# Gate steps in sparse attention, and where a chunked scan computes its decays and norm factors

## The chip, the core and the metric

The kernel runs on one core of a Trainium2 chip. A core has five engines that run their own instruction streams side by side: TensorE (PE in the profile; its weight loads are PEld), VectorE (DVE), ScalarE (ACT), GpSimd (POOL) and SyncE (SP), which here issues nearly all DMAs. They meet through semaphores, in SBUF (on-chip memory) and in PSUM (the banks that TensorE accumulates into). The metric is the device time of one execution in microseconds (us).

## What is computed

One layer of a hybrid decoder: three token mixers side by side on the same normalised input (a Mamba-2 scan, stick-breaking attention, sparse attention), merged by sigmoid gates, then a convolved gated MLP. SEQ is 1024, D_MODEL 1024, one batch. What the change touches of the reference:

```python
def ssd_chunked(x, dt, a, bmat, cmat):      # 8 chunks of 128 tokens, 4 groups of 4 heads
    def step(state, inp):
        x_c, dt_c, b_c, c_c = inp
        acum = jnp.cumsum(dt_c * a, axis=1)
        seg = acum[:, :, None] - acum[:, None, :]
        decay = jnp.exp(jnp.where(tri, seg, -jnp.inf))
        cb = jnp.einsum('btgn,bsgn->btsg', c_c, b_c)
        w = cb[..., None] * decay * dt_c[:, None]
        y = jnp.einsum('btsgh,bsghp->btghp', w, x_c)
        y = y + jnp.einsum('btgn,bghpn->btghp', c_c, state) * jnp.exp(acum)[..., None]
        ...
# after it, per group of 256 channels:
    yg = yg * lax.rsqrt(jnp.mean(yg * yg, axis=-1, keepdims=True) + NORM_EPS)

# sparse attention, per query: 64 compressed keys give an importance for 16 blocks of 64 keys
        imp_pad = jnp.pad(p_cmp.sum(axis=2), ((0, 0), (0, 0), (0, 0), (1, 0)))
        imp = (imp_pad.reshape(bsz, g, NSA_QBLK, nb, ratio).sum(axis=-1)
               + jnp.pad(imp_pad[..., ratio::ratio], ((0, 0), (0, 0), (0, 0), (0, 1))))
        imp = jnp.where(valid, jnp.where(forced, BIG, imp), NEG)
        _, idx = lax.top_k(imp, n_sel)

# merge
    gm = jax.nn.sigmoid(merge_gate).reshape(bsz, s, 3, D_MODEL)
    mixed = gm[:, :, 0] * (y_ssm @ w_br_ssm) + gm[:, :, 1] * (y_sb @ w_br_sb) + gm[:, :, 2] * (y_nsa @ w_br_nsa)
```

## The kernel before

Activations are channel-major: a tile is 128 channels by 512 tokens (one half of the sequence). A float32 product is made of three passes on TensorE, with each operand split into a rounded part and a remainder (`hi`, `lo`): hi·hi, hi·lo, lo·hi. A **unit** is 128 output channels of the input projection: two halves, each 8 steps (one per 128 input channels) of three 128x512 matmuls into a PSUM bank named `dense`. `load_w` (L263) fetches a unit's weights by SP, ScalarE makes `whi` (L270), GpSimd `wlo` (L271).

The program runs through stages: the normalised input and the token-major projections; sparse attention (`nsa_stage`); stick-breaking attention (`sb_stage`, four heads); the scan (`ssd_stage`, four groups q of 8 chunks c); the merge, the output projection and the MLP (`tail_stage`). The 24 units of the merge gates depend on nothing but the input and are needed only in the tail, so they serve as **fill**: `Fill.take(n)` puts n of their steps between the matmuls of a stage. `N_GATES`, `SB_GATES` and `SSD_GATES` (L165 to L167) say how many gate units each stage gets. A gate unit ends each half with three ScalarE operations (the sigmoid, L245 to L247) and a store to DRAM.

**Sparse attention.** The outer loop (L944) goes over n. In one turn it interleaves three coroutines: the scores and values of query block n (`attend`), the row maxima of block n+1 (`maxima`) and the compressed branch of block n+2 (`compressed`). Blocks are (g, i): two head groups, eight query blocks i. TensorE's order in this stage is the order of the code; other engines are ordered by the Tile scheduler, as everything is in the later stages. Per inner step, the loop takes two fill steps where no key block is due (`b is None`), else one if the two other coroutines had nothing to do (L976 to L979). Query block i has i+1 key blocks in the selected branch and min(i,4)+1 in the windowed one; the loop has at least `NSA_SLOTS` = 9 inner steps, so from i = 4 on (10 to 13 key blocks) no inner step is without one. `maxima` ends with a transpose of the running maxima through PSUM and a copy into rows 96 to 127 of Q1 (L861 to L863); the next turn's first score needs them. `compressed` exponentiates and normalises scores against 64 compressed keys (`cp`), from i = 4 on reduces them to the importance of 16 blocks and picks eight (L784 to L796), transposes `cp`, copies it out (`pT`, L803), multiplies it with the compressed values into the same PSUM bank (L807) and multiplies the result by its gate into `yacc` (L809). The bank `ps_b` has one buffer.

**The scan.** For group q, `front(c)` makes the decays of a chunk (L1167): DMA brings `cum`, the cumulated log decays of four heads broadcast over partitions; VectorE subtracts the row's own value and clips at 0, one operation of 128x128 per head (L1174); ScalarE exponentiates the four together (L1176); GpSimd multiplies with C·B into `W` (L1198) and makes `Cd` (L1181). Four TensorE operations go into `ps_t` (two buffers), read by `cb`, `xdt`, `Bt` and `xe` (L1194 to L1204). `back(c)` multiplies into `ps_b` and `ps_o`, updates `state` (L1225) and the rows of x (L1228). After each chunk `fill.take` gives two halves of units (one in the last group): the projection of the next group, then gates. Dense halves of the projection rotate over three banks, two of `psd` and one `ps_s` (class `Banks`); gate halves use `psd` alone. At the end of a group `rsqrt_mean` (L235) makes the norm factors: Ln and Exp by ScalarE into SBUF, then one Newton step by VectorE, all tiles but the first source in SBUF, and L1248 multiplies them into the rows.

## Time and profile before

| what | value |
|---|---|
| time, median of 3 runs | 2200.53 us (2199.61 to 2202.32) |
| the profiled execution's own time | 2200.72 us |
| its span, first to last instruction | 2199.0 us |
| mean granted TensorE clock | 0.994 |
| VectorE busy | 1352.9 us (62%) |
| ScalarE busy | 1264.8 us (58%) |
| GpSimd busy | 1094.2 us (50%) |
| sparse attention, about | 195 to 525 us of the span |
| stick-breaking attention, about | 525 to 907 us |
| scan, about | 907 to 1250 us |

The profile lists for each instruction its start and duration, and for an engine that sat idle the instruction that ended the wait ("idle before, releaser"). Durations of neighbouring instructions overlap: a 128x512 matmul shows 0.39 us, but the next one starts 0.23 us later. So start-to-start times are used for what work costs, and the idle column for what a wait costs.

### The profile page before, as it was taken

The numbers are of one execution on the slowest core, as the hardware profiler recorded it, in microseconds if no ns is written. First come the engines' busy times: TensorE is split into PE (matmuls) and PEld (weight loads), VectorE is DVE, ScalarE is ACT, GpSimd is POOL, SyncE is SP. The second block draws the span as 40 slices with busy tenths as digits, with TensorE's granted clock in tenths as the row PEclk, the third lists the DMA queues.
The fourth block names the chain that finished last, engine by engine and source line by source line (L and its number), as shares of the span: only waits on it lengthen the run. The fifth ranks groups of instructions, "written<-read, shape, count | busy, mean of one in ns | idle before, by whom it ended". The sixth has DMA issues, their size and how long they took to land. (4 is left out here: it accounts for less than half of the span.)

```text
span 2199.0 us, 30216 instructions
## 1 busy us (share of the span) xinstructions
PE 2139.4 (97%) x10697; PEld 1739.8 (79%) x10697; DVE 1352.9 (62%) x2538; ACT 1264.8 (58%) x2328; POOL 1094.2 (50%) x797
## 2 busy tenths in 40 slices
PE   7999999999999999999999899999999999999997
PEld 7997666767887878777887688888888888888887
DVE  8433774672277676848486743326876666666677
ACT  7134676666466677655555422135686666676564
POOL 3212576566233333343434427455577777765753
PEclk9999999999999999999999999999999999999999
DMA  5223212200201111222222455244444444486533
GB/s 199 85 84 94 68 37 68 72 13 30 66 34 53 48 41 46 82 82 82 73 81 87 139 208 184 96 141 166 140 139 158 163 144 149 136 275 200 186 114 115
DMA packets 127079, 240.73 MB, mean 109 GB/s; under 512 B 29328, under 2 KB 43472, under 8 KB 126928
## 3 DMA queue, kind: packets, MB, share of 16 engines
q1 hardware_dynamic: 126064, 238.06, 33.2%
q8 instruction: 84, 1.38, 0.3%
q10 hardware_dynamic: 864, 0.75, 0.1%
q14 instruction: 67, 0.55, 0.1%
HBM read 179.45 MB, written 59.31 MB: 109 GB/s over the span
## 5 line engine op out<-in xcount | busy, mean ns | idle before, releaser
L271 POOL TENSOR_TENSOR wlo<-wraw,whi 128x1024 fp32r<-128x1024 f32 (+1 forms) x118 | 273.8, 2322 | 403.8 <-ACT whi L270 379.9
L206 PE MATMUL dense<-h_hi,whi 128*128 128x512 f32 x896 | 361.2, 403 | 2.7 <-ACT sa L1070 2.7
L206 PE MATMUL dense<-h_hi,wlo 128*128 128x512 f32 x896 | 352.2, 393 | 0.0
L206 PE MATMUL dense<-h_lo,whi 128*128 128x512 f32 x896 | 351.7, 393 | 0.0
L270 ACT ACTIVATE whi<-wraw 128x1024 fp32r<-128x1024 f32 (+1 forms) x118 | 117.8, 999 | 186.6 <-PE dense L206 156.3
L887 POOL TENSOR_TENSOR wT_lo<-wT,wT_hi 128x512 fp32r<-128x512 f32 x132 | 168.9, 1290 | 87.2 <-ACT wT_hi L886 77.1
L206 PEld LDWEIGHTS dense<-h_hi,whi 128*128 128x128 f32 x896 | 169.3, 189 | 38.7 <-ACT sa L1070 3.1
L206 PE MATMUL dense<-lo,whi 128*128 128x512 f32 x512 | 199.5, 390 | 0.0
L206 PE MATMUL dense<-hi,whi 128*128 128x512 f32 x512 | 199.4, 392 | 0.0
L206 PE MATMUL dense<-hi,wlo 128*128 128x512 f32 x512 | 197.8, 389 | 0.0
L206 PEld LDWEIGHTS dense<-h_hi,wlo 128*128 128x128 f32 x896 | 168.9, 188 | 36.3 <-issue 0.5
L206 PEld LDWEIGHTS dense<-h_lo,whi 128*128 128x128 f32 x896 | 169.3, 189 | 32.2 <-issue 0.9
L1087 POOL TENSOR_TENSOR s_lo<-sa,s_hi 128x512 fp32r<-128x512 f32 (+2 forms) x48 | 53.8, 1125 | 151.1 <-ACT s_hi L1086 148.1
L206 PE MATMUL dense<-x,uhi 128*128 128x512 f32 x360 | 116.7, 389 | 0.0
L876 ACT ACTIVATE wT<-ps_s 128x512 f32<-128x512 f32 x132 | 78.5, 595 | 63.7 <-PE ps_s L206 58.9
L206 PEld LDWEIGHTS dense<-hi,whi 128*128 128x128 f32 x512 | 96.1, 188 | 20.7 <-issue 0.7
L206 PEld LDWEIGHTS dense<-lo,whi 128*128 128x128 f32 x512 | 96.1, 188 | 20.7 <-issue 0.7
L206 PEld LDWEIGHTS dense<-hi,wlo 128*128 128x128 f32 x512 | 96.1, 188 | 20.5 <-issue 0.5
L316 DVE SCALAR_TENSOR_TENSOR u<-dense,pv,u 128x511 f32<-128x511 f32 (+1 forms) x140 | 102.0, 741 | 5.4 <-ACT u L312 4.2
L886 ACT ACTIVATE wT_hi<-wT 128x512 fp32r<-128x512 f32 x132 | 82.2, 629 | 16.6 <-POOL wT L878 15.1
L206 PE MATMUL ps_s<-Q,K 128*128 128x512 f32 x264 | 83.6, 398 | 4.3 <-DVE Q L863 4.1
L1198 POOL TENSOR_TENSOR W<-dec,cb 128x512 f32<-128x512 f32 x32 | 42.5, 1334 | 81.6 <-DVE cb L1194 49.6
(483 smaller groups left out, 5798.7 us busy)
## 6 DMA issues: line engine op xcount, KB each, us to landing
wraw<-in_wfm SPq DMA_DIRECT2D x62, 512.0 KB, 3.7
wraw<-in_wup SPq DMA_DIRECT2D x52, 512.0 KB, 3.8
g_d<-gate_e SPq DMA_DIRECT2D x48, 256.0 KB, 2.1
ge<-g_d SPq DMA_DIRECT2D x24, 512.0 KB, 3.9
m_d<-u SPq DMA_DIRECT2D x44, 256.0 KB, 2.1
u<-m_d SPq DMA_DIRECT2D x36, 256.0 KB, 3.2
wraw<-in_wdn SPq DMA_DIRECT2D x33, 256.0 KB, 3.1
cum<-acum_d SPq DMA_DIRECT2D x32, 256.0 KB, 3.5
```

What stands on the lines that cost most here:

```text
L206: i = f(*a, **k)
L270: act(hi, raw, AF.Copy)
L271: (eng or (V if tiles else P)).tensor_tensor(lo, raw, fl(hi), op=OP.subtract)
L316: end = V.scalar_tensor_tensor(o[:, d:], ps[:, :512 - d], taps[d], o[:, d:], op0=OP.mult, op1=OP.add)
L876: act(w.rearrange("p h q -> p (h q)"), pz, AF.Exp)
L886: act(hi, wf, AF.Copy)
L887: P.tensor_tensor(lo, wf, fl(hi), op=OP.subtract)
L1087: (P if SB_SLO else V).tensor_tensor(s_lo[:, c0:], a[:, c0:], fl(s_hi[:, c0:]), op=OP.subtract)
L1198: P.tensor_tensor(W, dec, cb[:, None, :].to_broadcast([128, 4, 128]), op=OP.mult)
```

## The change

- `N_GATES` is 13 instead of 12. The cuts of the later stages move by one; stick-breaking attention keeps one gate unit for each of its first three heads, and the scan's group q = 1 has one gate unit instead of two.
- In a turn of the sparse loop with more than nine key blocks, two fill steps are taken ahead of the first score. `compressed` yields True for i < 4 between the copy `pT` and the product that reads it, and the loop then takes one more step there.
- The importance of the 16 blocks is one reduction over overlapping windows of five (stride four) of a buffer with four zero columns behind it, in place of a reduction over four, an addition of the neighbour and a multiplication by a mask; the mask that is added (0, 1e30 or -1e30) stays.
- The decays' difference is made by ScalarE: Relu(acum - cum) for each head, and the exponential takes the opposite sign.
- In groups q < 3 of the scan, the norm factors are made in the PSUM bank that holds the sum of squares, and multiplied into the rows half by half. The last group keeps `rsqrt_mean`.

```diff
-N_GATES = 12
-SB_GATES = (12, 13, 14, 15, 15)
-SSD_GATES = (15, 17, 19, 20, 24)
+N_GATES = 13
+SB_GATES = (13, 14, 15, 16, 16)
+SSD_GATES = (16, 18, 19, 20, 24)
...
+    imps = [wk.tile([128, 68], F32, name=f"imp{n}", bufs=1) for n in range(2)]
+    for t in imps:
+        P.memset(t, 0.0)
...
+    def windows(imp):
+        w = imp[:, 0:64].rearrange("p (b r) -> p b r", r=4)
+        return bass.AP(tensor=w.tensor, offset=w.offset, ap=[list(w.ap[0]), list(w.ap[1]), [1, 5]])
...
-            imp = wk.tile([128, 64], F32, name="imp")
-            V.tensor_reduce(imp, p.rearrange("p h n -> p n h"), axis=AX, op=OP.add)
+            imp = imps[i % 2]
+            V.tensor_reduce(imp[:, 0:64], p.rearrange("p h n -> p n h"), axis=AX, op=OP.add)
             im = wk.tile([128, 16], F32, name="im")
-            iv = imp.rearrange("p (b r) -> p b r", r=4)
-            V.tensor_reduce(im, iv, axis=AX, op=OP.add)
-            V.tensor_tensor(im[:, 0:15], im[:, 0:15], iv[:, 1:16, 0], op=OP.add)
-            V.tensor_tensor(im, im, fa[:, i, 0, :], op=OP.mult)
+            V.tensor_reduce(im, windows(imp), axis=AX, op=OP.add)
             V.tensor_tensor(im, im, fa[:, i, 1, :], op=OP.add)
...
         act(pT.rearrange("p a b -> p (a b)"), pt[:, :256], AF.Copy)
-        yield
+        yield i < 4
...
+        if nb > NSA_SLOTS:
+            fill.take(NSA_FILL[0])
         for m, b in enumerate(blocks):
...
-            idle = next(ga, 0) == 0
+            step = next(ga, 0)
+            idle = step == 0 and step is not False
...
-            fill.take(NSA_FILL[0] if b is None else NSA_FILL[1] + idle)
+            fill.take((NSA_FILL[0] if b is None else NSA_FILL[1] + idle) + (step is True))
...
             for h in range(4):
-                V.tensor_scalar(dec[:, h, :], cum[:, h, :], E.acum[:, c, 4 * q + h:4 * q + h + 1], 0.0,
-                                op0=OP.subtract, op1=OP.min)
-            act(dec, dec, AF.Exp)
+                act(dec[:, h, :], cum[:, h, :], AF.Relu, scale=-1.0, bias=E.acum[:, c, 4 * q + h:4 * q + h + 1])
+            act(dec, dec, AF.Exp, scale=-1.0)
...
-            E.rsqrt_mean(z1[:, s], z0[:, s], ps, 256)
+            if q == 3:
+                E.rsqrt_mean(z1[:, s], z0[:, s], ps, 256)
+                continue
+            v = z1[:, s]
+            V.tensor_scalar(v, ps, 1.0 / 256, EPS, op0=OP.mult, op1=OP.add)
+            act(ps, ps, AF.Ln, scale=1.0 / 256, bias=E.eps)
+            act(ps, ps, AF.Exp, scale=-0.5)
+            V.tensor_tensor(v, v, ps, op=OP.mult)
+            V.scalar_tensor_tensor(v, v, -0.5, ps, op0=OP.mult, op1=OP.mult)
+            V.scalar_tensor_tensor(ps, v, 1.5, ps, op0=OP.add, op1=OP.mult)
+            for n in range(2):
+                V.scalar_tensor_tensor(xs[n][:, s], xs[n][:, s], pvc(PV_SSM, 2 * q + n), ps, op0=OP.mult,
+                                       op1=OP.mult)
         for n in range(2):
-            V.scalar_tensor_tensor(xs[n], xs[n], pvc(PV_SSM, 2 * q + n), z1, op0=OP.mult, op1=OP.mult)
+            if q == 3:
+                V.scalar_tensor_tensor(xs[n], xs[n], pvc(PV_SSM, 2 * q + n), z1, op0=OP.mult, op1=OP.mult)
```

**Where instructions move.** TensorE, sparse attention, the start of the turn for query block 4 of the first head group. Before: the transposes of the maxima (`top`) stand directly ahead of the first score, whose operands are the tiles Q1 and Q2 and the keys K.

```order
L206 MATMUL ps_o<-wT_hi,V_hi 65x512
L206 MATMUL ps_o<-wT_hi,V_lo 65x512
L206 MATMUL ps_o<-wT_lo,V_hi 65x512
L206 MATMUL ps_t<-tab,top_1811 128x128 x4
L206 MATMUL ps_s<-Q_2674,K_0_1078 128x512
L206 MATMUL ps_s<-Q_2675,K_0_1080 128x512
```

The same place with the change:

```order
L206 MATMUL ps_t<-tab,top_1815 128x128 x4
L206 MATMUL dense<-h_hi,whi 128x512
L206 MATMUL dense<-h_lo,whi 128x512
L206 MATMUL dense<-h_hi,wlo 128x512
L206 MATMUL dense<-h_hi,whi 128x512
L206 MATMUL dense<-h_lo,whi 128x512
L206 MATMUL dense<-h_hi,wlo 128x512
L206 MATMUL ps_s<-Q_2687,K_0_1078 128x512
L206 MATMUL ps_s<-Q_2688,K_0_1080 128x512
```

Two steps of a gate unit, six matmuls, stand between the transposes and the score that waits for their copy. This happens in the eight turns of i = 4 to 7 in both head groups; in the eight of i = 0 to 3 one step comes between the transpose of `cp` and its product with VC. Those 24 steps are 8 that stood behind the stage's last attention step before, and the 16 of the thirteenth unit.

VectorE at the start of the scan, group q = 0, chunks 0 to 2, before (`dec` the decays, the `row` lines with `dense` or `ps_s` the convolution of the group's own projection, `xe` the operand that frees a `ps_t` bank):

```order
L1228 SCALAR_TENSOR_TENSOR row_8511<-row_8511,pv,ps_o 128x128
L1228 SCALAR_TENSOR_TENSOR row_8722<-row_8722,pv,ps_o 128x128
L1196 TENSOR_TENSOR xdt<-ps_t,dt_t 128x256
L1174 TENSOR_SCALAR dec<-cum,acum 128x128 x4
L540 SCALAR_TENSOR_TENSOR row_9615<-ps_s,pv,halo 128x3
L542 SCALAR_TENSOR_TENSOR row_9615<-ps_s,pv,row_9615 128x511
L1204 TENSOR_TENSOR xe<-ps_t,dte 128x256
```

and with the change:

```order
L1234 SCALAR_TENSOR_TENSOR row_8557<-row_8557,pv,ps_o 128x128
L1234 SCALAR_TENSOR_TENSOR row_8768<-row_8768,pv,ps_o 128x128
L1202 TENSOR_TENSOR xdt<-ps_t,dt_t 128x256
L528 TENSOR_TENSOR row_9538<-row_9538,half 128x512
L540 SCALAR_TENSOR_TENSOR row_9661<-ps_s,pv,halo 128x3
L1210 TENSOR_TENSOR xe<-ps_t,dte 128x256
```

The four `dec` operations between `xdt` and `xe` are gone from VectorE, as are sixteen ahead of them. On ScalarE they stand here, with the change (`dec` from `cum` is the Relu, `dec` from `dec` the exponential, `half` the sigmoid of the projection's SiLU):

```order
L1208 ACTIVATE Bt<-ps_t 128x128 x2
L1181 ACTIVATE dec<-cum,acum 128x128 x8
L1182 ACTIVATE dec<-dec 128x512
L534 ACTIVATE row_9661<-dense,pv 128x512
L536 ACTIVATE halo<-dense,pv 128x3
L1182 ACTIVATE dec<-dec 128x512
L1185 ACTIVATE cum<-cum 128x512
L245 ACTIVATE half<-row_9538 128x512
L1181 ACTIVATE dec<-cum,acum 128x128 x4
L246 ACTIVATE half<-half 128x512
L1181 ACTIVATE dec<-cum,acum 128x128 x4
L1182 ACTIVATE dec<-dec 128x512
```

The first two chunks' eight Relus stand together ahead of an eviction of the projection (`row` from `dense`); the next eight come between the operations of a sigmoid. No instruction that loads an activation table is added.

## The prediction, made before the changed kernel was run

> **What bounds the kernel now.** First the page and the busy time by stage, to see which engine sets the time and where it is not busy.

> ```profile
> span 2199.0 us, 30216 instructions
> PE 2139.4 (97%) x10697; PEld 1739.8 (79%) x10697; DVE 1352.9 (62%) x2538; ACT 1264.8 (58%) x2328; POOL 1094.2 (50%) x797
> ...
> 195.00:525.00 330.00, 316.21 (x1739) 227.33 (x1738) 211.08 (x538) 215.94 (x409) 199.79 (x192) 1.00 0.17 50
> ...
> 907.00:1250.00 343.00, 332.49 (x1831) 264.90 (x1830) 236.30 (x546) 180.99 (x309) 142.62 (x87) 1.00 0.28 89
> ```

> In the window rows the second number is the stretch, the third TensorE's busy time. TensorE is the bound: it idles 2199.0 - 2139.4 = 59.6 us. The change removes no matmul from it; it moves gate steps and shortens what other engines do. So it can win no more than TensorE waits in the stages it touches: 330 - 316.2 = 13.8 us in sparse attention, 343 - 332.5 = 10.5 us in the scan. Next, who ended those waits (total, times, longest), first sparse attention, then the scan:

> ```profile
> PE ps_s L206 <- DVE Q L863: 4.1, 4, 1.3
> PE ps_b L206 <- ACT pT L803: 3.0, 4, 1.0
> PE ps_b L206 <- DVE yacc L809: 1.9, 2, 1.0
> ...
> PE ps_b L206 <- DVE state L1225: 5.0, 4, 1.7
> PE ps_t L206 <- DVE xe L1204: 4.2, 1, 4.2
> PE ps_o L206 <- DVE row L1228: 1.3, 1, 1.3
> ```

> The first two are the places where the change inserts steps; the third is behind the importance on VectorE; the last three are the scan's whole idle time.

> **Gate steps ahead of scores and behind the copy pT.** One of the four pT waits on TensorE's timeline, with the dense steps behind it:

> ```profile
> 229.28 0.39 PE L206 MATMUL ps_b<-tab,cp 128*128 128x128 f32 x2
> 230.67 0.71 PE L206 MATMUL ps_b<-VC,pT 128*128 128x128 f32 x4 [1.01 <-ACT pT L803]
> 231.14 0.48 PE L206 MATMUL dense<-h_hi,whi 128*128 128x512 f32 x1
> 231.46 0.40 PE L206 MATMUL dense<-h_lo,whi 128*128 128x512 f32 x1
> 231.69 0.39 PE L206 MATMUL dense<-h_hi,wlo 128*128 128x512 f32 x1
> ```

> A step costs 3 x 0.23 = 0.69 us; the first dense matmul behind another kind takes 0.32 instead of 0.23, so a new place for a step costs about 0.09 us more. One step covers 0.69 us of each of four pT waits (3.0 us in all, longest 1.0): about 2.5 us go, 0.5 stay. Two steps, 1.38 us, cover each of four score waits (4.1 us, longest 1.3): 4.1 us go, or 3.9 where a copy comes a little later. Sixteen new places cost 16 x 0.09 = 1.4 us. The steps themselves are no extra work: 8 of the 24 come from the stage's end, 16 from the scan's second group, where they ran without a wait before.

> The 24 steps are three halves of units: nine sigmoid operations, one and a half weight splits by ScalarE and by GpSimd, three stores and one or two weight loads on SP's queue, all earlier than before. ScalarE is busy 215.9 of 330 us here and GpSimd 199.8, so there is room; what queues behind a sigmoid operation is a pT, Q or score copy for up to some 0.6 us. I charge 0.5 us for all of it, with bounds 0 and 4 (eight turns by one such operation less what their own two steps cover).

> **Importance.** VectorE, in the turn that makes one of the two yacc waits:

> ```profile
> 267.64 0.52 DVE L788 TENSOR_TENSOR im<-im,imp 128x15 f32<-128x15 f32 x1
> 268.42 0.99 DVE L789 TENSOR_TENSOR im<-im,fa 128x16 f32<-128x16 f32 x1
> 270.58 0.41 DVE L809 TENSOR_TENSOR yacc<-ps_b,sg 128x256 f32<-128x256 f32 x1
> 271.24 0.16 DVE L792 MAX8 top<-im 128x8 f32<-128x16 f32 x1
> ...
> 271.85 0.15 DVE L794 MATCH_REPLACE8 left<-top,im 128x16 f32<-128x16 f32 x1
> ...
> 271.04 0.66 PE L206 MATMUL ps_b<-tab,qd 128*128 128x128 f32 x4 [0.96 <-DVE yacc L809]
> ```

> L788 and L789 go: 1.5 us ahead of yacc here. In the new order the maximum and the replacement come ahead of it instead, 0.16 + 0.15 and some 0.1 to load the values to match, so yacc comes about 1.1 us earlier and the 0.96 us go; 1.6 of the two waits' 1.9 us is my value, bounds 0 and 1.9. The reduction reads 80 numbers instead of 64, at nothing: VectorE is not waited for there.

> Sparse attention: 2.5 + 3.9 + 1.6 - 1.4 - 0.5 = **6.1 us** gained, bounds 1 and 10.

> **Decays by ScalarE.** The largest single wait, with the engines around it:

> ```profile
> 919.45 2.38 POOL L271 TENSOR_TENSOR wlo<-wraw,whi 128x1024 fp32r<-128x1024 f32 x1 [0.31 <-ACT whi L270]
> 921.79 1.26 POOL L1198 TENSOR_TENSOR W<-dec,cb 128x512 f32<-128x512 f32 x1
> 923.01 1.26 POOL L1181 TENSOR_TENSOR Cd<-cum,row 128x512 f32<-128x512 f32 x1
> ...
> 919.61 4.94 DVE L1174 TENSOR_SCALAR dec<-cum,acum 128x128 f32<-128x128 f32 x4
> ...
> 925.85 0.90 PE L206 MATMUL ps_t<-tab,row 128*128 128x128 f32 x3 [4.18 <-DVE xe L1204]
> ...
> 920.00:930.00 10.00, 5.82 (x34) 4.59 (x33) 9.93 (x20) 5.62 (x13) 4.27 (x3) 0.83 0.28 80
> ...
> L1174 DVE TENSOR_SCALAR dec<-cum,acum x128: 269/276/2393, 907.0 to 1235.1; 128x128 f32<-128x128 f32 x128
> ...
> L1174 DVE TENSOR_SCALAR dec<-cum,acum 128x128 f32<-128x128 f32 x128 | 60.4, 525 | 7.2 <-POOL W L1198 6.5 <-DMA cum<-acum_d 0.7
> ```

> Four decays take 4.94 us where 4 x 0.276 (the median) would be 1.1: they last as long as GpSimd's three operations beside them. xe waits behind them in VectorE's queue, and TensorE's transposes wait for xe's bank: 4.18 us. After the wait TensorE runs slower for a while: its granted clock is 0.83 over these 10 us (the number after the five engines), so another 10 x 0.17 = 1.7 us are lost. Without the decays VectorE has nothing of that kind ahead of xe: 16 more that stood before are gone too, at 0.525 us some 8 us. What is late next is W, by way of ScalarE: its eight first Relus. They have no row; the nearest are these:

> ```profile
> L1202 ACT ACTIVATE Bt<-ps_t 128x128 f32<-128x128 f32 x28 | 7.2, 269 | 7.7 <-PE ps_o L206 4.2 <-DVE xdt L1196 3.5
> L1096 ACT ACTIVATE sz<-sz 128x256 f32<-128x256 f32 x16 | 6.7, 418 | 0.0
> L1096 ACT ACTIVATE sz<-sz 128x512 f32<-128x512 f32 x24 | 15.1, 628 | 1.7 <-DVE sz L1095 0.9
> ```

> A 128x128 copy out of PSUM takes 0.27 us; from SBUF, 0.42 at 256 columns is the upper bound, and less 128 x (628 - 418) / 256 it is 0.31, my value. A chunk's four take 1.2 us (1.1 to 1.7). VectorE took 1.1 at best and 2.1 on average, so W comes no later, and in the new order 20 dense matmuls stand between the first two products with W. I count the 4.2 + 1.7 = **5.9 us** as gained, bounds 2 and 6.

> [...]

> **Norm factors in PSUM.** They count in the last group, where VectorE still makes those of the group before. Its Newton step and the end of the scan on TensorE:

> ```profile
> 1210.09 2.89 DVE L240 TENSOR_TENSOR row<-row,row 128x512 f32<-128x512 f32 x1
> ...
> 805.75 0.68 DVE L1073 TENSOR_TENSOR sa<-ps_s,sa 128x512 f32<-128x512 f32 x1
> ...
> 1213.89 0.67 PE L206 MATMUL ps_b<-xe,Bt 128*128 128x256 f32 x2 [0.80 <-DVE state L1225]
> 1223.65 0.67 PE L206 MATMUL ps_b<-xe,Bt 128*128 128x256 f32 x2 [1.38 <-DVE state L1225]
> ...
> 1236.21 0.70 PE L206 MATMUL ps_b<-xe,Bt 128*128 128x256 f32 x2 [1.12 <-DVE state L1225]
> 1239.65 0.67 PE L206 MATMUL ps_b<-xe,Bt 128*128 128x256 f32 x2 [1.71 <-DVE state L1225]
> 1242.67 0.66 PE L206 MATMUL ps_o<-W,xdt 128*64 128x128 f32 x8 [1.33 <-DVE row L1228]
> ```

> L240 with both sources in SBUF took 2.89 us; the same shape with one source in PSUM takes 0.68 (L1073). With 2.2 us from there, and each chunk's decays, the first two waits (0.80 and 1.38) go. The last three have no gate step left between chunks: PSUM product, state, product again. The fourth and fifth, 3.0 us, stay; of the third, half goes. **2.8 us** gained, bounds 0 and 6.3.

> **What is taken away.** Group q = 1 loses a gate unit, 16 x 0.69 = 11 us of cover for its end and the start of q = 2. Group q = 2 has had one gate unit before, and at its end TensorE's wait column is empty until 1213.89; so I cost it at little. But both ps_s banks are now held until their half is multiplied into the rows: six VectorE operations of L1073's size, 4.1 us a half, 8.2 for both, and states and rows are queued between. The third bank of the next group's projection is one of them, and in the new order 32 dense matmuls (7.4 us) and two chunks' products stand ahead of its first use. I charge **1 us**, bounds 0 and 5 (a 3 us wait with the slower matmuls behind it).

> The stages before and behind keep their order up to noise: the stick-breaking stage's waits and the tail's I take as they are.

> **The sum**: 6.1 + 5.9 + 2.8 - 1.0 = 13.8 us. From the profiled execution's own 2200.72 us (span 2199.0 and 1.7 around it), which is the median of the runs shown plus 0.2: 2186.9, so 2186.7 for a median, say **2187 us**. About 0.2% (4.4 us) is what a measurement can tell from no change.

> **Rivals.**
> - All waits at these places go, those at the scan's end too: 13.8 + 10.5 + 1.7 less the 1.4 of new places: 2176 us. For it: steps give every engine slack. Against: the scan's end has nothing to put between.
> - The waits of sparse attention are moved, not removed: VectorE is so busy from i = 4 on that the next score or transposes wait instead. For: five smaller kinds of wait stand behind the three shown, 13.8 - 9.0 = 4.8 us. Gain 1 there: 2192 us.
> - The ps_s banks hold up the projection at two group ends, 4 us each: 2194 us. For: by the terms above there is hardly a margin. Against: only every third bank is one, and TensorE has other work in its queue ahead of it.
> - Slower: ScalarE becomes the scan's bound. In the last group the decays' 1.2 us a chunk join exponentials, gates and weights:

> ```profile
> 1200.00:1240.00 40.00, 34.99 (x216) 26.61 (x216) 34.26 (x86) 22.64 (x40) 20.73 (x15) 1.00 0.31 106
> ```

> ScalarE (sixth number) is busy 22.6 of 40 us; five chunks add 6, leaving 11 free. It decides if evictions queued behind Relus free banks later by over 1 us in most of 32 chunks: 24 us lost, and the scan's 8.7 not gained, 6.1 kept: some 2218 us; half of that would be 2206. [...]

> **Chances.** Forecast 0.56 (2181 to 2192); all waits go 0.12; moved waits 0.13; banks 0.11; ScalarE 0.08. Faster by over 0.2% (under 2196): all of the first two, most of the next two, 0.87; same 0.07; slower 0.06. The range, 2177 to 2196, reaches from the first rival to just behind the third, and leaves out the slower case and the edges.

> **What the next profile would show.** Right: the waits for Q L863 and yacc gone, hardly a pT wait left; stick-breaking attention starting about 5 us later (11 of the thirteenth unit less 6.1), the scan ending about 14 earlier; no wait over 2 us between 907 and 1200; the fourth and fifth wait at the scan's end still there. Wrong: dense waits ended by ScalarE (half, gate_e) in the scan, a ps_s matmul waiting for VectorE, or the score waits still there with steps ahead of them.

## The result, and the profile after

The changed kernel takes 2177.83 us (median of 4 runs, 2176.78 to 2178.68) against 2200.56 us before on the same chips: ratio 0.9895, 95% interval 0.9882 to 0.9908, so 22.7 us less. A later set of runs of it gave 2177.89 us, 0.9897 (0.9883 to 0.9910). The forecast was 2187 us, 13.8 us less.

The head of the page of the profiled execution (2176.78 us), as it was shown of before:

```profile
span 2174.9 us, 30180 instructions
PE 2133.0 (98%) x10697; PEld 1736.5 (80%) x10697; DVE 1287.2 (59%) x2400; ACT 1301.7 (60%) x2456; POOL 1093.7 (50%) x799
```

TensorE runs the same 10697 matmuls. VectorE has lost 65.7 us of busy time and ScalarE has gained 36.9: 128 decays that cost VectorE 60.4 us have gone to ScalarE.

Next, what TensorE waited for in sparse attention (195 to 523 us; total, times, longest), changed kernel:

```profile
PE ps_o L206 <- ACT oT L904: 1.2, 5, 0.4
PE ps_t L206 <- DVE mx L856: 1.1, 2, 0.6
PE ps_b L206 <- DVE cp L785: 1.0, 1, 1.0
PE ps_t L206 <- DVE top L856: 0.9, 3, 0.4
```

The scores' waits for Q (4.1) and the waits for pT (3.0) and yacc (1.9) are gone, all of them. Only mx has grown by more than 0.1 us (0.3 before). The same view of the scan, with nothing left out:

```profile
PE ps_o L206 <- DVE row L1234: 1.3, 1, 1.3
PE ps_b L206 <- DVE state L1231: 0.9, 1, 0.9
```

10.5 us of waits have become 2.2; both that are left are at the scan's end, at 1215 and 1218 us.

Where the 24.1 us between the two spans lie is read from TensorE's timeline, at the first operation of each stage: the first transposes of `q_in`, the first stick-breaking score, the first product with `W`, the last group of products with `Cd`. Before:

```profile
169.99 0.38 PE L206 MATMUL ps_b<-tab,q_in 128*128 128x128 f32 x2
590.01 0.87 PE L206 MATMUL ps_s<-row,row 128*128 128x256 f32 x6
913.39 0.66 PE L206 MATMUL ps_o<-W,xdt 128*64 128x128 f32 x8
1243.13 0.64 PE L206 MATMUL ps_o<-Cd,state 128*64 128x128 f32 x8
```

After:

```profile
168.82 0.38 PE L206 MATMUL ps_b<-tab,q_in 128*128 128x128 f32 x2
587.89 0.87 PE L206 MATMUL ps_s<-row,row 128*128 128x256 f32 x6
909.34 0.66 PE L206 MATMUL ps_o<-W,xdt 128*64 128x128 f32 x8
1218.92 0.64 PE L206 MATMUL ps_o<-Cd,state 128*64 128x128 f32 x8
```

| stretch | before | after | moved unit | gained | forecast |
|---|---|---|---|---|---|
| to the first `q_in` | 170.0 | 168.8 | | 1.2 | 0 |
| **sparse stretch**, `q_in` to the first score | 420.0 | 419.1 | +10.9 | 11.8 | 6.1 |
| first score to the scan | 323.4 | 321.5 | | 1.9 | 0 |
| **scan**, first `W` to last `Cd` | 329.7 | 309.6 | -10.9 | 9.3 | 7.7 |
| to the end | 955.9 | 956.0 | | -0.1 | 0 |

The thirteenth unit is 48 matmuls of 0.227 us more in the sparse stretch, and as many fewer in the scan. Below, the scan is counted to the start of the last matmul, 0.36 us later: 330.1 before and 309.9 after.

### The profile page after: what moved, and what is told of

Same layout as the page of the kernel before. It is cut to its first block, busy times and chain, and to the rows that moved or that the text cites. A ratio compares the mean times of both kernels' runs of the same rounds, so it can differ in the third digit from the quotient of the medians.

```text
span 2174.9 us, 30180 instructions
## 1 busy us (share of the span) xinstructions
PE 2133.0 (98%) x10697; PEld 1736.5 (80%) x10697; DVE 1287.2 (59%) x2400; ACT 1301.7 (60%) x2456; POOL 1093.7 (50%) x799
## 3 DMA queue, kind: packets, MB, share of 16 engines
q8 instruction: 84, 1.38, 0.3%
## 4 chain that ended last, share of the span: by engine, by line
PE 92%; DVE 3%; ACT 3%; issue 1%; POOL 0%; DMA 0%; DVEq 0%; ACTq 0%; POOLq 0%
PE dense L206 69%; PE ps_s L206 9%; PE ps_o L206 6%; PE ps_t L206 5%; PE ps_b L206 2%; ACT wT L880 0%; ACT wT_hi L890 0%; ACT h_hi L402 0%; DVE mx L856 0%; DVE sz L1064 0%; PE psn L206 0%; DVE x L1893 0%; ACT sq L408 0%; DVE sa L1075 0%; DVE sa L1090 0%
## 5 line engine op out<-in xcount | busy, mean ns | idle before, releaser
L271 POOL TENSOR_TENSOR wlo<-wraw,whi 128x1024 fp32r<-128x1024 f32 (+1 forms) x118 | 271.5, 2303 | 401.6 <-ACT whi L270 363.2
L206 PE MATMUL dense<-h_hi,whi 128*128 128x512 f32 x896 | 360.4, 402 | 2.7 <-ACT sa L1077 2.7
L206 PE MATMUL dense<-h_hi,wlo 128*128 128x512 f32 x896 | 351.6, 392 | 0.0
L206 PE MATMUL dense<-h_lo,whi 128*128 128x512 f32 x896 | 350.9, 392 | 0.0
L270 ACT ACTIVATE whi<-wraw 128x1024 fp32r<-128x1024 f32 (+1 forms) x118 | 117.9, 1000 | 193.6 <-PE dense L206 158.9
L891 POOL TENSOR_TENSOR wT_lo<-wT,wT_hi 128x512 fp32r<-128x512 f32 x132 | 168.8, 1290 | 83.4 <-ACT wT_hi L890 72.4
L206 PE MATMUL dense<-lo,whi 128*128 128x512 f32 x512 | 199.5, 390 | 0.0
L206 PE MATMUL dense<-hi,whi 128*128 128x512 f32 x512 | 199.4, 392 | 0.0
L206 PEld LDWEIGHTS dense<-h_hi,whi 128*128 128x128 f32 x896 | 168.7, 188 | 38.0 <-ACT sa L1077 3.1
L206 PE MATMUL dense<-hi,wlo 128*128 128x512 f32 x512 | 197.8, 389 | 0.0
L206 PEld LDWEIGHTS dense<-h_hi,wlo 128*128 128x128 f32 x896 | 168.2, 188 | 36.9 <-issue 1.2
L206 PEld LDWEIGHTS dense<-h_lo,whi 128*128 128x128 f32 x896 | 168.6, 188 | 31.4 <-issue 0.8
L206 PE MATMUL dense<-x,uhi 128*128 128x512 f32 x360 | 116.7, 389 | 0.0
L206 PEld LDWEIGHTS dense<-lo,whi 128*128 128x128 f32 x512 | 96.1, 188 | 20.8 <-issue 0.7
L206 PEld LDWEIGHTS dense<-hi,whi 128*128 128x128 f32 x512 | 96.1, 188 | 20.8 <-issue 0.7
L206 PEld LDWEIGHTS dense<-hi,wlo 128*128 128x128 f32 x512 | 96.1, 188 | 20.4 <-issue 0.5
L206 PE MATMUL ps_s<-Q,K 128*128 128x512 f32 x264 | 83.4, 397 | 0.2 <-ACT wT L880 0.2
L206 PEld LDWEIGHTS dense<-x,uhi 128*128 128x128 f32 x360 | 67.6, 188 | 14.0
```

Of the source, the lines that this page charges most:

```text
L206: i = f(*a, **k)
L270: act(hi, raw, AF.Copy)
L271: (eng or (V if tiles else P)).tensor_tensor(lo, raw, fl(hi), op=OP.subtract)
L891: P.tensor_tensor(lo, wf, fl(hi), op=OP.subtract)
```

## The experiments

Each changes one thing, in the kernel before (one part alone) or in the changed kernel (one part undone, or one number). The table has all of them; the ratio is to the kernel before on the same chip, with its 95% interval. The two stretches are those of each kernel's one profile. Half clock means a stretch in which TensorE's granted clock in the trace is 0.5; by that share, work that fills 3.4 us at it would take 1.7 us at full clock. (In the trace of before, 128x512 matmuls start 0.427 us apart at half clock, from 806.0 to 809.4 us, and 0.227 us apart behind it.)

| kernel | median us | ratio | sparse stretch | scan |
|---|---|---|---|---|
| before | 2200.53 | 1 | 420.0 | 330.1 |
| changed | 2177.83 | 0.9895 (0.9882 to 0.9908) | 419.1 | 309.9 |
| gate steps alone | 2197.51 | 0.9985 (0.9976 to 0.9994) | 422.9 | 325.8 |
| importance alone | 2196.76 | 0.9984 (0.9975 to 0.9993) | 416.2 | 331.2 |
| decays by ScalarE alone | 2194.92 | 0.9972 (0.9962 to 0.9982) | 419.8 | 322.0 |
| norm factors in PSUM alone | 2201.12 | 0.9996 (0.9987 to 1.0005) | 419.9 | 330.0 |
| changed, decays undone | 2196.96 | 0.9984 (0.9975 to 0.9993) | 419.1 | 324.1 |
| changed, norm factors undone | 2183.56 | 0.9920 (0.9907 to 0.9934) | 419.1 | 312.2 |
| changed, 12 gate units | 2184.55 | 0.9929 (0.9916 to 0.9941) | 414.7 | 320.2 |
| before, decays to PSUM | 2205.39 | 1.0023 (1.0014 to 1.0032) | 419.9 | 330.1, with 22 matmuls more |
| changed, gate halves behind 7 chunks | 2178.93 | 0.9903 (0.9890 to 0.9917) | 419.1 | 318.8 |
| changed, gate halves behind 6 chunks | 2181.40 | 0.9911 (0.9897 to 0.9924) | 419.1 | 314.5 |

### One part alone: the gate steps

```diff
-N_GATES = 12
+N_GATES = 13
...
-        yield
+        yield i < 4
...
+        if nb > NSA_SLOTS:
+            fill.take(NSA_FILL[0])
```

> The kernel before with the gate steps alone: the 13th gate unit, the 16 new places and the shifted cuts; importance, decays and norm factors as they were. Theory A (sizes as in the prediction, the idle column is what a wait costs): the score and pT waits go for 3.9 + 2.5 us and the new places cost 1.4, so the stretch from the first q_in transpose to the first stick-breaking score grows by 10.9 - 5.0 = 5.9 us, and the run is about 4 us faster (5.0 less the 1.0 for the unit that leaves q=1). Theory B (a wait costs what the start-to-start distance shows, and all of them go): 5.2 + 4.1 - 1.5 = 7.8, the stretch grows by 3.1 and the run is 6 to 8 us faster. Theory C (the gain beyond the forecast comes from the lighter VectorE of the importance part): the pT waits of the steps i >= 4 stay, and the stretch grows by 6 us or more. The first transpose of the yacc places (1.9 us of idle time) stays in all three.

Measured: the sparse stretch grew by 2.9 us, a gain of 8.05 where the forecast had 5.0: theory B. The Q and pT waits are gone, yacc's stay. How a wait's price is read decides here. TensorE's timeline of before around one score wait:

```profile
467.51 0.60 PE L206 MATMUL ps_t<-tab,top 128*128 128x128 f32 x4
469.28 0.71 PE L206 MATMUL ps_s<-Q,K 128*128 128x512 f32 x2 [1.17 <-DVE Q L863]
```

and of the changed kernel at the same place, where a step stands behind the transposes:

```profile
469.10 0.60 PE L206 MATMUL ps_t<-tab,top 128*128 128x128 f32 x4
469.45 0.48 PE L206 MATMUL dense<-h_hi,whi 128*128 128x512 f32 x1
```

The next operation starts 1.77 us after the transposes with the wait and 0.35 without it: the wait cost 1.42, not the 1.17 of the idle column. The column counts from the modelled end of the last transpose (0.60), but the next matmul can start 0.25 ahead of that end (469.45 against 469.70 here). By the starts of the last transpose and the next matmul, 0.03 us apart where nothing waits, the four Q waits cost 5.04 us instead of 4.1, the four pT waits 3.96 instead of 3.0.

But the scan of this kernel got worse: 325.8 + 10.9 = 336.7, that is 6.6 us lost. Its waits there:

```profile
PE ps_b L206 <- DVE state L1228: 5.0, 4, 1.7
PE ps_t L206 <- DVE xe L1207: 4.6, 1, 4.6
PE dense L206 <- DVE row L542: 2.4, 1, 2.4
PE ps_o L206 <- DVE row L1231: 1.3, 1, 1.3
PE ps_s L206 <- DVE row L238: 1.1, 1, 1.1
```

The third and the fifth are new, at 1122 and 1106 us: the end of the second group, which has lost one of its gate units. Of the 8 us won in one stage 6.6 are given back in another, half of it as half clock, and the run gains 3.5 where theory B had 6 to 8. By the starts of the same matmuls in both kernels 1.5 of the 6.6 lie at 925 us, where 6.8 us at half clock follow the wait instead of 3.4; the other 5.1 come from the end of the second group on.

### One part alone: the importance

```diff
-            V.tensor_reduce(im, iv, axis=AX, op=OP.add)
-            V.tensor_tensor(im[:, 0:15], im[:, 0:15], iv[:, 1:16, 0], op=OP.add)
-            V.tensor_tensor(im, im, fa[:, i, 0, :], op=OP.mult)
+            V.tensor_reduce(im, windows(imp), axis=AX, op=OP.add)
```

> The kernel before with the importance by one overlapping sum alone, 12 gate units. Theory A (idle column): the waits of the first transpose of qd go, -1.6 to -1.9 us in the stretch from the first q_in transpose to the first stick-breaking score (420.0 us before). Theory B (start-to-start): -2.4 us. Theory C (an interplay with the gate steps): under 1 us alone, since the score and pT waits beside it stay and take up the time. The score and pT waits stay in A and B. Nothing changes behind 590 us but by the state of the clock.

Measured: 3.85 us gained in the sparse stretch, more than any theory had. The waits (the first two rows, and the one that grew, 0.3 before):

```profile
PE ps_s L206 <- DVE Q L867: 3.9, 4, 1.2
PE ps_b L206 <- ACT pT L807: 3.0, 4, 1.0
...
PE ps_t L206 <- DVE mx L856: 1.1, 2, 0.6
```

yacc's two waits are gone, Q's and pT's are not: it is no interplay with the gate steps. By the distance from each matmul to the next, summed by pair, the transposes of `qd` behind a score gained 2.44 us (theory B's size), and 0.86 came from the row maxima's products, which follow 32 masked ones; the rest is spread in amounts of up to 0.5 us of both signs. The 0.86 are 0.03 us for each of 32, too little for a row of the waits; that VectorE frees their banks sooner is only inferred.

8.05 + 3.85 is 11.9, the 11.8 of the whole change in this stretch. Here the parts add.

### One part alone: the decays, and the norm factors

```diff
-                V.tensor_scalar(dec[:, h, :], cum[:, h, :], ..., 0.0, op0=OP.subtract, op1=OP.min)
-            act(dec, dec, AF.Exp)
+                act(dec[:, h, :], cum[:, h, :], AF.Relu, scale=-1.0, bias=...)
+            act(dec, dec, AF.Exp, scale=-1.0)
```

> The kernel before with the four Relu of the decays on ScalarE alone. Theory A (prediction): the 4.2 us wait at 925 us and the stretch at half clock behind it go, 5.9 us; the five waits at the end of the scan stay, so the scan (330.1 us from the first product of W to the last of Cd) becomes 324.2. Theory B (VectorE's long decays also made the late norm factors late): the waits at the scan's end shrink too, and the scan comes to 319 to 322, a gain of 8 to 11. Theory C (ScalarE becomes the bound): Relu at 0.39 us x4 a chunk delays W and the scan gains under 3.

Measured: the scan gained 8.1 us. The 4.2 us wait and its half clock are gone, 5.7 us by the starts of the same matmuls on both sides, and 2.4 more came behind that, at the scan's end: theory B, at the edge of its range. Its waits in the scan, all:

```profile
PE ps_b L206 <- DVE state L1224: 2.8, 1, 2.8
PE ps_o L206 <- DVE row L1227: 1.3, 1, 1.3
```

The second of these experiments has the last part of the diff alone:

```diff
-            E.rsqrt_mean(z1[:, s], z0[:, s], ps, 256)
+            if q == 3: ...                                   # as before
+            act(ps, ps, AF.Ln, scale=1.0 / 256, bias=E.eps)
+            act(ps, ps, AF.Exp, scale=-0.5)
+            ...
```

> The kernel before with the norm factors in PSUM alone (quarters 0 to 2). Theory A (prediction): of the five waits at the scan's end the first two and half the third go, -2.8 us, and the held ps_s banks cost up to 0.5: the scan becomes 327.3 to 327.8. Theory B (the late factors come from VectorE's decays, not from the norm): under 1 us, the five waits stay. Theory C (norm in PSUM is what took the first four waits): -4 to -5, scan 325 to 326. The 4.2 us wait at 925 us stays in all three.

Measured: no difference. Its waits for `state` shrank from 5.0 to 3.8 us:

```profile
PE ps_b L206 <- DVE state L1225: 3.8, 2, 2.4
```

But a longer stretch at half clock behind the wait at 925 us (6.8 us instead of 3.4) took the same away again. Alone the part is worth under 2 us, between theories A and B.

The four parts alone gain 3.5 + 4.2 + 6.0 - 0.2 = 13.6 us, the whole 22.7. The 9 us between them are more than the intervals of these runs (about 2 us each way) explain; an interplay was the likely reason, and the loss of the gate steps alone in the scan said where to look.

### One part undone: the decays back on VectorE

The changed kernel without the hunk on the decays.

> The changed kernel with the decays back on VectorE, all else as changed. Theory A (the parts add): the 8.1 us that the scan gained with ScalarE's decays alone come back, the scan (309.9 us after the change) becomes 318, the run about 2184 to 2186. Theory B (the unit taken out of the second quarter needs the shorter decays): beside the wait near 925 us and the half clock behind it, a wait of about 2.4 us comes in the quarter that lost its gate unit, as it did in the kernel with the gate steps alone, so the scan becomes 321 to 325 and the run 2189 to 2193. The stretch from the first q_in transpose to the first stick-breaking score stays at 419 in both.

Measured: 19.1 us slower than the changed kernel, though the part alone had brought 6.0. Theory B: the scan is in its range, the run beyond it. All of its waits in the scan:

```profile
PE ps_t L206 <- DVE xe L1211: 4.0, 1, 4.0
PE ps_b L206 <- DVE state L1232: 3.7, 2, 2.3
PE ps_b L206 <- DVE xe L1211: 2.6, 1, 2.6
PE ps_o L206 <- DVE row L1235: 1.3, 1, 1.3
PE ps_s L206 <- DVE row L1264: 0.8, 1, 0.8
```

The wait of 2.6 us is at 1109 us, where the second group has a unit fewer. The timeline there, across engines:

```profile
1103.23 2.39 POOL L271 TENSOR_TENSOR wlo<-wraw,whi 128x1024 fp32r<-128x1024 f32 x1
...
1104.55 2.37 DVE L1181 TENSOR_SCALAR dec<-cum,acum 128x128 f32<-128x128 f32 x2
...
1105.57 1.27 POOL L1188 TENSOR_TENSOR Cd<-cum,row 128x512 f32<-128x512 f32 x1
...
1109.02 0.70 PE L206 MATMUL ps_b<-xe,Bt 128*128 128x256 f32 x2 [2.62 <-DVE xe L1211]
```

Two decays, 0.28 us each when nothing holds them, last 2.37 us, until GpSimd's second operation ends at 1106.84. The profiled execution (2192.28 us) is this kernel's fastest; its other ten have a lower mean clock (0.989 to 0.992 against 0.993), so they ran longer at half clock. Where, no profile shows.

### One part undone: the norm factors

The changed kernel without the last hunk, that on the norm factors.

> The changed kernel with the norm factors in SBUF as before, all else as changed. Theory A (the norm part is worth what it gave alone, 0 to 1.7 us): the scan becomes 310 to 312, the run 2178 to 2180. Theory B (it matters once the other parts are in): a wait at the scan's end of about 2.8 us, as in the kernel with ScalarE's decays alone, in place of 0.9, and a wait for a ps_s bank of about 1 us in the quarter that lost a unit: the scan becomes 313 to 314, the run 2181 to 2182.

Measured: 5.7 us slower. The scan lost 2.3 us: the wait for `state` at its end is 2.8 us instead of 0.9, as theory B had it, but no wait for `ps_s` came, so the scan lies between the two theories, and the run beyond both. Behind the 2.8 us TensorE ran 6.8 us at half clock (3.4 us lost, part of it behind the scan), and near 804 us another 3.4 us (1.7 lost), which the last section puts down to phase. Of its four runs one, at a mean clock of 0.996, was only 1.8 us slower than the change.

```profile
PE ps_b L206 <- DVE state L1231: 2.8, 1, 2.8
PE ps_o L206 <- DVE row L1234: 1.2, 1, 1.2
```

### The places without the unit

```diff
-N_GATES = 13
-SB_GATES = (13, 14, 15, 16, 16)
-SSD_GATES = (16, 18, 19, 20, 24)
+N_GATES = 12
+SB_GATES = (12, 13, 14, 15, 15)
+SSD_GATES = (15, 17, 19, 20, 24)
```

> The changed kernel with the 16 new places but 12 gate units and the cuts of before. Theory A (a place needs a step to put there): the steps run out 16 places earlier in the sparse stage, the waits that lie behind come back for 1 to 4 us, and the run is 2179 to 2182; the second quarter of the scan keeps its two units. Theory B (the order alone brings the gain): the same time as the change within 1 us, 2177 to 2179. The stretch from the first q_in transpose to the first stick-breaking score is 408.2 (419.1 less a unit of 10.9) in B and 409 to 412 in A.

Measured: 6.7 us slower than the change, and the sparse stretch 414.7 us, both beyond theory A's ranges. The steps do run out earlier, as theory A says, but what comes uncovered is neither a score nor a pT: it is the preparation of the scan's sums at the end of the stage (562 and 565 us), with 6.8 us at half clock there. Another 3.4 us at half clock near 800 us are the same matter as at 804 us above.

```profile
PE dense L206 <- DVE row L1018: 1.9, 1, 1.9
PE ps_b L206 <- DVE dte L990: 1.2, 1, 1.2
```

So the thirteenth unit pays for the places, and ScalarE's decays pay for its going from the scan.

### What makes a decay long: the result in PSUM

```diff
+            pd = ps_s().rearrange("p (h n) -> p h n", h=4)
-                V.tensor_scalar(dec[:, h, :], cum[:, h, :], ...)
-            act(dec, dec, AF.Exp)
+                V.tensor_scalar(pd[:, h, :], cum[:, h, :], ...)
+            act(dec, pd, AF.Exp)
```

> The kernel before with the decays still on VectorE, but written to a bank of PSUM, from which ScalarE's Exp takes them. Every one of the 31 long decays of the kernel before (over 400 ns of 128) began while a GpSimd instruction ran and ended 81 to 86 ns behind its end. Theory A (VectorE is held by GpSimd when it writes these decays from SBUF to SBUF): with the result in PSUM no decay is held, the longest is under 500 ns, the wait at 925 us and its half clock go as with ScalarE's Relu, and the scan comes from 330.1 to 322-324. Theory B (VectorE simply has too much work there, and only taking the decays away helps): decays of 300 ns or more x128 stay on VectorE, some still long, the wait at 925 us stays within 1 us, the scan 328 to 331. The ps_s bank it takes may cost up to 1 us in either.

Measured: slower by 4.6 us as a whole, but the question is answered. The line of its decays (minimum, median, maximum in ns), and of the Relus in the changed kernel:

```profile
L1175 DVE TENSOR_SCALAR ps_s<-cum,acum x128: 333/345/356, 905.3 to 1240.5; 128x128 f32<-128x128 f32 x128
```

```profile
L1181 ACT ACTIVATE dec<-cum,acum x128: 385/389/421, 902.9 to 1210.3; 128x128 f32<-128x128 f32 x128
```

No decay is long any more; before, the range was 269 to 2393 ns. The work stayed on VectorE, and 64 of the 128 began while a GpSimd operation ran; only the place of the result is another. The wait of 4.2 us for xe at 925 us is gone with its half clock; 0.8 us for `state` is left there. Theory A, then, for the decays. For the time it fails. The 330.1 us of the scan can't be set beside the 330.1 of before, since 22 matmuls that came ahead of the first product with `W` now come behind it; from the first score to the last `Cd`, where both run the same ones, it is 655.7 us against 653.5. What the 925 us wait gave is lost ahead of that first product: there TensorE waits 1.5, 0.9 and 2.6 us (901 to 909 us), with 3.4 us at half clock behind. The longest of the three is the price of the place: the four decays now hold a `ps_s` bank that a projection half wants. The waits from 900 us on, the first two rows:

```profile
PE ps_b L206 <- DVE state L1226: 4.7, 5, 2.4
PE ps_s L206 <- ACT dec L1177: 2.6, 1, 2.6
```

### Two versions beyond the change

The two waits left at the scan's end (0.9 and 1.3 us) have no gate step near them. `SSD_LAST`, the chunks of the last group that get a half behind them, was set from 5 to 7, and to 6.

> A version beyond the change: the changed kernel with a gate half behind each of the first seven chunks of the last quarter, not five. Theory A: the halves lie where PE still waits at the scan's end (0.9 and 1.3 us), the first of these waits goes and the second may, -1 to -2.5 us, the scan (less two halves of 5.5 us that move into it) gains as much, run 2175.5 to 2177. Theory B: the halves that are taken from behind the scan were the cover of the last quarter's norm and of the loads for the tail, the stretch from the scan to the tail grows by a new wait of as much, and the run stays at 2177 to 2179.

> A version beyond the change: the changed kernel with a gate half behind each of the first six chunks of the last quarter. With seven, PE waited 1.7 us for the sum of squares behind the scan, since one half was left to cover it. Theory A (the optimum lies between): the first of the two waits at the scan's end goes (0.9 us), two halves still cover the sum of squares, -1 us, 2176 to 2177.5. Theory B (the cover is needed whole): a wait of up to 1 us for the sum of squares, no gain within 0.5 us.

Measured: neither beats the change. With 7 both waits went and the scan gained 2.0 us beside the two halves moved into it, but TensorE then waited 1.7 us for the sum of squares (`row`, GpSimd): theory B. With 6 one wait went, 0.9 us; in the profiled execution waits for weights of 1.4 us in all came in the tail, none for the sum of squares, and the median is 3.5 us above the change: neither theory. What makes up the rest of that is open. TensorE's waits with 7, from the scan into the tail:

```profile
PE ps_s L206 <- POOL row L1247: 1.7, 1, 1.7
PE dense L206 <- POOL wlo L271: 0.6, 1, 0.6
```

### The changed kernel once more

> The changed kernel once more, with a new profile. Theory A (half clock behind PE's wait of 2.7 us near 803 us depends on the phase of the throttle's windows, not on the kernel): the wait is there again, with or without a stretch at half clock, and the stick-breaking stage takes 308.0 us without it or 309.7 with one of 3.4 us; the stages but for that within 0.2 us of the first profile. Theory B (the change itself keeps the clock up): no half clock there again.

Measured: the stages are the first profile's within 0.2 us, but for the start, where the first `q_in` came at 170.4 instead of 168.8 us. The wait near 803 us is there (2.72 us), with no half clock behind it: alone this fits both theories. The other runs decide: of the variants of the changed kernel two have half clock there (norm factors undone, 12 units), and of those of the kernel before three have none (gate steps, importance, norm factors alone). It is theory A; the last section has the numbers.

## Why the prediction was right in kind and short in size

**The direction and the places were right.** Each wait that the forecast wanted gone is gone, and no wait over 2 us is left between 907 and 1200 us. Of the rivals the first, all waits go (2176 us), came nearest: it holds in sparse attention, while at the scan's end two waits stayed. The other three did not come: no score wait was moved, no `ps_s` matmul waits for VectorE, nobody waits for the Relus. What failed is the size of terms. The 2177.83 us lie outside the band that the forecast gave its own case (2181 to 2192) and 0.8 us inside the range's lower edge. Two of its signs came out otherwise: stick-breaking attention starts 2.1 us earlier, not 5 later, and the scan ends 24.2 us earlier, not 14.

**Waits of sparse attention (2.5 + 3.9).** The term priced waits by the idle column. Start to start they were 4.0 + 5.0 us, and no rest was left of pT's, where 0.5 was to stay. In the longest pT wait a sigmoid operation of a gate half stood ahead of pT in ScalarE's queue (timeline of before):

```profile
229.73 0.62 ACT L247 ACTIVATE gate_e<-gate_e 128x512 f32<-128x512 f32 x1
230.25 0.38 ACT L803 ACTIVATE pT<-ps_b 128x256 f32<-128x256 f32 x1
```

The moved steps put that half's end elsewhere: in the changed kernel only the copy `wT` stands there ahead of pT. The 1.4 us for new places was near: 9.0 us of waits went and 8.05 were gained, so they and ScalarE's earlier work, charged at 0.5, cost 1.0 together. (Seven smaller kinds of wait stood behind the three shown, not five as the second rival has it.)

**Importance (1.6).** 3.85: the qd transposes gave 2.44 by the same reading error, and the rest is spread in pieces too small for the waits view, its cause inferred only. The bound of 1.9 was wrong for that reason, and the stretch's upper bound of 10 fell with it (11.8).

**Decays by ScalarE (5.9).** The wait at 925 us with its half clock was worth 5.7, as forecast. The Relu took 0.389 us, not 0.31, inside its bounds (0.27 to 0.42); four take 1.6 us, and nobody waited. Not foreseen: 2.4 us more at the scan's end.

That GpSimd's operations hold the decays was read right from a single row, and the lengths now show it. In the kernel before, 31 of 128 decays took over 400 ns; each of them began while a GpSimd operation ran and ended 80 to 86 ns behind the end of one; none of the 97 short ones began so. With the result in PSUM, 64 began beside a GpSimd operation and none took over 356 ns. So here a decay with source and result in SBUF that began beside a GpSimd operation lasted until that one's end; what in the chip makes it wait is not in these traces. By the median VectorE is the quicker one for a decay (276 ns against the Relu's 389), by the mean the slower (525).

**Norm factors (2.8) and what is taken away (-1.0).** These two terms were split wrongly. Alone the norm factors bring under 2 us, and alone the loss of a gate unit costs 5.1 to 6.6, not 1. In the whole the waits at the scan's end fell from 6.3 to 2.3 us, the fourth too (0.9 left at that place, where 1.7 were to stay), and the lost unit cost nothing, because the long decays had gone from VectorE's queue there as well: with them back, waits of 2.6 and 0.8 us came there. The forecast did not ask what its decays term does for the term behind it. And it read the 2.89 us of L240 as the price of sources in SBUF, where it is the longest of eight:

```profile
L240 DVE TENSOR_TENSOR row<-row,row x8: 678/688/2892, 993.0 to 1259.5; 128x512 f32<-128x512 f32 x8
```

The median is what L1073 takes with a source in PSUM. It is the decays' story once more: of the 24 operations of the Newton step in the kernel before (L240 to L242) five began while a GpSimd operation ran and took 0.96 to 2.89 us, the other 19 took 0.68 to 0.69; of the 18 with an operand in PSUM in the changed kernel 13 began so, and all took 0.67 to 0.69.

That the forecast's sum, 13.8, is near the sum of the four parts alone, 13.6, is chance: its terms are other ones.

**The clock (0).** 1.7 us of the gain is half clock near 806 us that the profile of before has and this one has not, and 1.2 us is a shorter start. The first lies in the stage that the forecast took as unchanged; neither comes from the change.

So of the 24.1 us between the two profiled executions 13.8 were forecast, 5.7 more came from sparse attention's terms and 1.6 more from the scan's; the other 3.0 lie in stages that the change leaves as they are. How much of that is in the 22.7 us between the medians is not shown.

## What to carry to other kernels

Price a wait by the distance between the starts on both sides, less the distance that is kept there when nothing waits, not by the idle column alone. Before an operation is kept on an engine for its median time, look at its longest: if these end with another engine's operations, moving it can free more than that median (here 276 ns, with a mean of 525 and a wait of 4.2 us behind four of them). And when a change takes cover away in one place and shortens work there in another part, put a price on the pair, since each part alone may bring little, or lose.

## What the runs showed that was not expected

TensorE's clock. Near 803 us there is in every one of the 13 profiles the same wait of 2.7 us, in code that no kernel changes. In five of them half clock follows, in eight not. Two of the windows, each 4 us (after the five engines comes the granted clock), first before, then after:

```profile
806.00:810.00 4.00, 4.00 (x13) 3.11 (x12) 3.87 (x8) 3.34 (x6) 0.80 (x1) 0.57 0.01 3
```

```profile
806.00:810.00 4.00, 4.00 (x21) 3.38 (x20) 3.89 (x8) 3.92 (x9) 2.26 (x2) 1.00 0.01 4
```
